# Rotary embedding on one core: storing each pair of batches in two halves of four rows

## The chip, the cores and the metric

One core of a Trainium2 chip. The metric is the device time of one execution in microseconds (us). The time of a run is 1.5 us more than its span in the profile, from the first to the last instruction (169.03 against 167.5 in the profile). Executions come in two states. A run is called slow when it is over 1.5% above the fastest of the same kernel; only fast runs are compared here. Ratios are the mean time of one kernel's fast runs over that of the other kernel's fast runs of the same rounds, so they are not quite the ratio of the medians that stand beside them.

Engines: PE is the matrix engine, DVE the vector engine, ACT the scalar engine, POOL the general one, SP the one that issues loads. "DMA engine" always means one of the 16 transfer engines.

## The reference

```python
batch, seq, dim = (16, 512, 1024)          # 16 heads of 64, float32
x = x.reshape(batch, seq, 16, 64)
x1, x2 = x[..., :32], x[..., 32:]
cos, sin = cos[None, :, None, :], sin[None, :, None, :]
out = np.concatenate([x1 * cos - x2 * sin, x1 * sin + x2 * cos], axis=-1)
```

33.55 MB come in and as much goes out; the arithmetic is two products and a sum per element.

## The kernel before

The work is cut into nine tiles: batch 0 alone (4 rows of 1024 numbers in each of 128 partitions), seven pairs of batches (8 rows), and batch 15 alone (4 rows). A row of a partition is 4 KB and the rows of a partition are contiguous in DRAM, so a pair moves as 128 descriptors (contiguous pieces) of 32 KB and a single batch as 128 of 16 KB. A transfer has landed when its semaphore has grown by 16, one for each DMA engine: the landing records of every transfer here have 16 entries. Five regions of 8 rows in on-chip memory are used in turn, so tile `t` is loaded into the region that tile `t - 5` has left.

```python
tiles = [(0, R1)] + [(b, R2) for b in range(1, batch - 1, 2)] + [(batch - 1, R1)]   # R1 = 4, R2 = 8
NT = len(tiles)
REGIONS = 5
...
loads = [(t, r, n) for t, (_, whole) in enumerate(tiles)
         for n in (R1 if t == 1 else whole,) for r in range(0, whole, n)]
...
def on_sync(sp):                                   # loads, in order
    for c, (t, r, n) in enumerate(loads):
        if t >= REGIONS:
            sp.wait_ge(sem_out[t - REGIONS], 16)   # the store that frees the region has landed
        sp.dma_start(in_sbuf(t, r, n), in_dram(x1, x2, t, r, n)).then_inc(sem_in[c], 16)
    ...                                            # (the two tables go behind the first load)
    sp.wait_ge(sem_rest, 16 * (NT - len(sem_out)))

def on_scalar(ae):                                 # copies of PE's sums, and stores
    ...
    for u in range(NU):
        t, r, k = where(u)
        if PE2[u]:
            ae.wait_ge(sem_e, n_pe[u])
            ae.activation(xs[:, k, :], t1_ps[:, u % NT1, :], COPY).then_inc(sem_a, 1)
        if r == tiles[t][1] - 1:                   # last row of the tile: store all of it
            wait_added(ae, u)
            ae.dma_start(in_dram(o1, o2, t, 0, r + 1), in_sbuf(t, 0, r + 1)).then_inc(
                sem_out[t] if t < len(sem_out) else sem_rest, 16)
```

Per row, POOL multiplies by the sine (`t2_sb`), DVE by the cosine (`t1_ps`), and DVE or PE adds them. Loads go out on SP's queue (`q1` in the profile), stores on ACT's queue (`q10`); while both hold work their packets take turns.

## Time and profile before

| | before |
|---|---|
| unprofiled runs | 161.96, 166.91, 161.80 us (median 161.96) |
| profiled run | slow state, 169.03 us, span 167.5 us |
| bytes | 67.26 MB, 402 GB/s over the span |
| POOL busy, DVE busy | 134.2 us, 131.0 us |

How to read it: POOL and DVE need some 132 us, the bytes need 156 us at the pace that the packets show, so the transfers set the length and what matters is whether the 16 DMA engines are ever without work.

### The profile page before, as it was taken

The numbers are of one execution on the slowest core, as the hardware profiler recorded it, in microseconds if no ns is written. First come the engines' busy times: TensorE is split into PE (matmuls) and PEld (weight loads), VectorE is DVE, ScalarE is ACT, GpSimd is POOL, SyncE is SP. The second block draws the span as 40 slices with busy tenths as digits, with TensorE's granted clock in tenths as the row PEclk, the third lists the DMA queues.
The fourth block names the chain that finished last, engine by engine and source line by source line (L and its number), as shares of the span: only waits on it lengthen the run. The fifth ranks groups of instructions, "written<-read, shape, count | busy, mean of one in ns | idle before, by whom it ended". The sixth has DMA issues, their size and how long they took to land.

```text
span 167.5 us, 565 instructions
## 1 busy us (share of the span) xinstructions
PE 70.2 (42%) x94; PEld 24.2 (14%) x94; DVE 131.0 (78%) x118; ACT 24.0 (14%) x26; POOL 134.2 (80%) x66
## 2 busy tenths in 40 slices
PE   6040039284937672476402907019390392700000
PEld 1020023022211211022101201013020130200000
DVE  0079996999999999999959994398964989999000
ACT  3020002211222040204020222002202022200000
POOL 5069999999999999999949994399954999996000
PEclk9999999855596789558985795855955559675555
DMA  5999999999899999999999999999999999488970
GB/s 160 420 425 431 474 423 387 438 434 446 384 485 384 479 391 470 385 470 407 446 415 430 438 391 477 399 462 407 470 399 419 427 470 415 172 376 376 442 317 23
DMA packets 3026, 67.26 MB, mean 402 GB/s; under 512 B 336, under 2 KB 592, under 8 KB 592
## 3 DMA queue, kind: packets, MB, share of 16 engines
q1 hardware_dynamic: 1728, 33.69, 47.6%
q10 hardware_dynamic: 1296, 33.56, 46.8%
q14 instruction: 2, 0.02, 0.0%
HBM read 33.69 MB, written 33.55 MB: 402 GB/s over the span
## 4 chain that ended last, share of the span: by engine, by line
DMA 48%; DVE 16%; POOL 11%; issue 7%; PE 7%; ACT 2%; SPq 0%; DVEq 0%; POOLq 0%
DMA x_sb<-in_x_dram 25%; DMA out_dram<-x_sb 19%; POOL t_sb L249 11%; DVE t_ps L285 8%; DVE x_sb L296 7%; PE t_ps L206 7%; DMA stage<-in_sin_dram 4%; ACT x_sb L171 2%; DVE t_sb L278 1%; SPq L155 0%; SPq L152 0%; ACT s_sb L161 0%; ACT s_sb L162 0%; POOLq L146 0%; DVEq L295 0%
## 5 line engine op out<-in xcount | busy, mean ns | idle before, releaser
L249 POOL TENSOR_TENSOR t_sb<-x_sb,s_sb 128x1024 f32<-128x1024 f32 x57 | 131.9, 2361 | 18.3 <-DMA x_sb<-in_x_dram 11.7
L206 PE MATMUL t_ps<-t_sb,ident 128*128 128x512 f32 x84 | 65.4, 935 | 68.9 <-POOL t_sb L249 48.6
L285 DVE TENSOR_TENSOR t_ps<-x_sb,pair_ps 128x1024 f32<-128x1024 f32 x56 | 67.5, 1222 | 14.4 <-DMA x_sb<-in_x_dram 11.0
L296 DVE TENSOR_TENSOR x_sb<-t_ps,t_sb 128x1024 f32<-128x1024 f32 x43 | 52.3, 1218 | 0.5 <-POOL t_sb L249 0.5
L206 PEld LDWEIGHTS t_ps<-t_sb,ident 128*128 128x128 f32 x84 | 22.3, 288 | 111.6 <-issue 59.6
L171 ACT ACTIVATE x_sb<-t_ps 128x1024 f32<-128x1024 f32 x21 | 21.5, 1024 | 113.2 <-PE t_ps L206 113.2
L285 DVE TENSOR_TENSOR t_ps<-x_sb,tab_ps 128x1024 f32<-128x1024 f32 x8 | 9.7, 1223 | 0.0
L278 DVE TENSOR_TENSOR t_sb<-x_sb,tab_ps 128x1024 f32<-128x1024 f32 x7 | 8.5, 1215 | 0.0
L256 DVE COPY tab_ps<-stage 128x128 f32<-128x128 f32 x1 | 0.3, 295 | 7.7 <-DMA stage<-in_cos_dram 7.7
L189 PE MATMUL pair_ps<-stage,pick 128*128 128x256 f32 x4 | 2.0, 667 | 5.2 <-DMA stage<-in_sin_dram 5.2
L182 PE MATMUL t_ps<-zero 128*128 128x512 bf16 x6 | 2.7, 630 | 1.3 <-DVE zero L254 1.3
L189 PEld LDWEIGHTS pair_ps<-stage,pick 128*128 128x128 f32 x4 | 1.2, 324 | 6.3 <-issue 6.1
L232 POOL TENSOR_SCALAR_AFFINE_SELECT pick<-pick 128x128 f32<-128x128 f32 x2 | 1.4, 706 | 0.1
L161 ACT ACT_TABLE_LOAD x1 | 1.3, 1283 | 0.8 <-PEq L329 0.8
L161 ACT ACTIVATE s_sb<-stage 128x128 f32<-128x128 f32 x1 | 0.3, 311 | 7.0 <-DMA stage<-in_sin_dram 7.0
L182 PEld LDWEIGHTS t_ps<-zero 128*128 128x128 bf16 x6 | 0.7, 137 | 2.4 <-DVE zero L254 1.2
L254 DVE MEMSET zero<- 128x256 uint32 x1 | 0.3, 272 | 0.9 <-PEq L329 0.9
L165 ACT ACTIVATE s_sb<-pair_ps 128x256 f32<-128x256 f32 x1 | 0.4, 384 | 1.7 <-PE pair_ps L189 1.7
L217 POOL MEMSET ident<- 128x128 f32 x1 | 0.2, 205 | 0.3 <-POOLq L329 0.3
L166 ACT ACTIVATE s_sb<-pair_ps 128x256 f32<-128x256 f32 x1 | 0.4, 377 | 0.0
L219 POOL TENSOR_SCALAR_AFFINE_SELECT ident<-ident 128x128 f32<-128x128 f32 x1 | 0.3, 297 | 0.1
L329 POOL MEMSET const-float32-0.0<- 128x1 f32 x1 | 0.1, 99 | 0.3 <-issue 0.3
(7 smaller groups left out, 1.3 us busy)
## 6 DMA issues: line engine op xcount, KB each, us to landing
out_dram<-x_sb ACTq DMA_DIRECT2D x7, 4096.0 KB, 31.9
x_sb<-in_x_dram SPq DMA_DIRECT2D x6, 4096.0 KB, 42.2
x_sb<-in_x_dram SPq DMA_DIRECT2D x4, 2048.0 KB, 13.8
out_dram<-x_sb ACTq DMA_DIRECT2D x2, 2048.0 KB, 15.8
stage<-in_cos_dram SPq DMA_DIRECT2D x1, 64.0 KB, 7.6
stage<-in_sin_dram SPq DMA_DIRECT2D x1, 64.0 KB, 7.3
```

The costliest lines, as they stand in the source:

```text
L161: ae.activation(s1_sb[:, :, 0, :], sv, COPY, scale=-1.0)
L165: ae.activation(s2[:, :, :, 0, :], pair_ps[:, :, 1, :, :], COPY, scale=-1.0)
L166: ae.activation(s2[:, :, :, 1, :], pair_ps[:, :, 1, :, :], COPY).then_inc(sem_s, 1)
L171: ae.activation(xs[:, k, :], t1_ps[:, u % NT1, :], COPY).then_inc(sem_a, 1)
L182: pe.matmul(t1_ps[:, k, b * BANK:(b + 1) * BANK], zero[:, 0:P], zero[:], start=True, stop=True).then_inc(sem_w, 1)
L189: pe.matmul(pair_ps[:, k].rearrange("p c r d -> p (c r d)"), pick[:, k].rearrange("q s b -> q (s b)"), stage[:].rearrange("q c f -> q (c f)"),
L206: ins = pe.matmul(t1_ps[:, u % NT1, b * BANK:(b + 1) * BANK], ident[:], t2[:, b * BANK:(b + 1) * BANK], start=False, stop=True, skip_group ...
L232: pl.affine_select(out=pick[:, k], in_=pick[:, k], compare_op=mybir.AluOpType.is_equal, fill=0.0, base=-k, pattern=[[-2, P // 2], [0, 2]], ...
L249: pl.tensor_tensor(t2_sb[:, u % NT2, :, :, :], swapped(k), over_heads(s_of(t, r)), mult).then_inc(sem_p, 1)
L278: ve.tensor_tensor(t2_sb[:, u % NT2, :, :, :], swapped(k), over_heads(v_ps), mult)
L285: ve.tensor_tensor(t1_ps[:, u % NT1, :].rearrange("p (h d) -> p h d", d=HALF), x_sb[:, k, :, :, :].rearrange("p h t d -> p (h t) d"), c_of ...
L296: ve.tensor_tensor(xs[:, k, :], t1_ps[:, u % NT1, :], t2_sb[:, u % NT2, :, :, :].rearrange("p h t d -> p (h t d)"), add,).then_inc(sem_v, 1)
```

## The change

Its intent is to let the first half of a pair leave while the second half is still being computed. The load of a pair stays one transfer with 32 KB descriptors.

```diff
                 if t >= REGIONS:
-                    sp.wait_ge(sem_out[t - REGIONS], 16)
+                    sp.wait_ge(sem_out[t - REGIONS], 16 * tiles[t - REGIONS][1] // R1)
...
-            sp.wait_ge(sem_rest, 16 * (NT - len(sem_out)))
+            sp.wait_ge(sem_rest, 16 * sum(n for _, n in tiles[len(sem_out):]) // R1)
...
-                if r == tiles[t][1] - 1:
+                if r % R1 == R1 - 1:
                     wait_added(ae, u)
-                    ae.dma_start(in_dram(o1, o2, t, 0, r + 1), in_sbuf(t, 0, r + 1)).then_inc(
+                    first = r + 1 - R1
+                    ae.dma_start(in_dram(o1, o2, t, first, R1), in_sbuf(t, first, R1)).then_inc(
                         sem_out[t] if t < len(sem_out) else sem_rest, 16
```

## The prediction

> **What bounds the kernel now.** I read the page first (busy shares, slices, queues), then the chain that ended last, then busy time by window, then the records of single DMA packets in the trace.
>
> ```profile
> PE 70.2 (42%) x94; PEld 24.2 (14%) x94; DVE 131.0 (78%) x118; ACT 24.0 (14%) x26; POOL 134.2 (80%) x66
> DMA  5999999999899999999999999999999999488970
> DMA packets 3026, 67.26 MB, mean 402 GB/s; under 512 B 336, under 2 KB 592, under 8 KB 592
> q1 hardware_dynamic: 1728, 33.69, 47.6%
> q10 hardware_dynamic: 1296, 33.56, 46.8%
> L249 POOL TENSOR_TENSOR t_sb<-x_sb,s_sb 128x1024 f32<-128x1024 f32 x57 | 131.9, 2361 | 18.3 <-DMA x_sb<-in_x_dram 11.7
> ```
>
> No engine is full: POOL 80%, DVE 78%. The 16 DMA engines are, in every slice but the last six. The store queue (q10) has 1296 packets: 9 stores of 128 partitions plus 16 completions is 9 x 144 = 1296, so **one packet is one row's descriptor**, 32 KB for a pair. In the packet records a 32 KB packet takes 1.213 us and a 16 KB one 0.611 us at the median, in either direction: 16 x 32768 B / 1.213 us = 432 GB/s for loads and stores together.
>
> ```profile
> 54.28 31.92 DMA out_dram<-x_sb
> 86.20 0.02 issue
> 86.22 41.54 DMA x_sb<-in_x_dram
> ```
>
> Columns are start, duration, what. The chain runs through a store of a pair, then the load that this store's landing releases (a region is reused five tiles later), and then POOL. 41.5 us for 4.2 MB is twice the 19.4 us that it needs at half the bandwidth, so it queued behind another load. From about 40 us on both queues are backlogged and alternate 1:1; landings of loads, and of stores, come some 20 us apart.
>
> ```profile
> 120.00:142.00 22.00, 10.19 (x12) 3.64 (x12) 17.63 (x16) 3.07 (x3) 17.83 (x9) 0.60 1.01 432
> 143.00:144.00 1.00, 1.00 (x2) 0.34 (x1) 1.00 (x2) 0.00 (x0) 1.00 (x1) 0.50 0.53 229
> 145.00:146.00 1.00, 0.53 (x2) 0.00 (x0) 1.00 (x2) 0.43 (x1) 1.00 (x1) 1.00 0.08 33
> 160.00:162.00 2.00, 0.00 (x0) 0.00 (x0) 0.00 (x0) 0.00 (x0) 0.00 (x0) 0.50 1.00 426
> 164.00:165.00 1.00, 0.00 (x0) 0.00 (x0) 0.00 (x0) 0.00 (x0) 0.00 (x0) 0.50 0.08 33
> ```
>
> The last two columns are the DMA share and GB/s. The reader is to see two holes, at 143 to 147 and after 163 us, in which the share is 0.08: **one engine of the 16** works while the others stand idle. The per-engine landings show it: 15 engines finish the load of the last pair by 122.5 us, one at 127.8; the last store by 163.1, one at 167.4. That engine's store packets took 1.25 to 1.85 us between 51 and 137 us; a lag of 3 us at 64 us grew to 9 us. But this profile is of the slow state (169.03 us; its span is 167.5, so 1.5 us lie outside). The fast runs took 161.8 and 161.96, and those count. I hold that the fast state is this picture without the late engine, which I can check: load of the last pair at 122.3, then 11 POOL rows at 2.31 (25.5 us) give 147.8, and the last store goes out at 149.2. The pair before it goes out at about 141.6, ahead of the end of the store in flight at 144.5 (its 15 good engines). So there is **no hole in the fast state**: 144.5 + 9.7 (8 packets of 1.213 of the last pair) + 4.9 (8 of 0.611) = 159.1, with 1.5 outside 160.6, against 161.8 measured.
>
> A second way gives the same. Packet durations summed over 16 engines are 158.2 us per engine; less some 0.6 us for the late engine, and started at 1.8 us, they end at 159.4, plus 0.3 for the landing and 1.5 outside: 161.2. The fast run is within 0.6 us of its DMA work.
>
> **What the Trainium skill says.** "DMA: Bandwidth & Descriptors", section "Queues, rings and completion order": each DMA engine goes round-robin between queue rows packet by packet, and finishes a packet before it switches. The trace agrees, with one descriptor to a packet: the first store (2 MB, 16 KB packets) ran beside 32 KB loads and landed at 39.4, 18.9 us after its issue; 8 turns of 0.611 + about 1.3 is 15.3 us plus some 2 of start. With equal bytes it would have been about 11.8. "Issuing engines are not separate DMA queues" says that all queues share the same 16 engines: here they sum to 432 GB/s, whichever runs. "Where 436 GB/s comes from" gives a ceiling of 435.2 GB/s; the 432 agree, so no arrangement of transfers can go much faster. "Why a DMA increments its semaphore by 16 and not by 1" warns of two DMAs in flight on one semaphore: only the total says that both landed. The change waits for that total (32), so a region still frees only when the second half has landed; no run shows the failure.
>
> **The change part by part.**
>
> Removed: seven stores of 128 descriptors of 32 KB. Added: fourteen of 16 KB. Bytes are the same. On each engine a pair's store goes from 8 x 1.213 = 9.70 us to 16 x 0.611 = 9.78, so 7 pairs cost 0.5 us more, all of it on the bound; seven more completions of 9 ns per engine are under 0.1. Seven more DMA issues on ACT at about 0.55 us are 3.9 us on an engine that is 14% busy; the first half is issued behind row 3, which ACT itself has just evacuated, so the wait there is met already. Path: 0.
>
> Moved, first: the first half of a pair goes out some 8 us earlier (half of a pair's 16.2 us on POOL). That gives DMA work earlier only where the store queue is empty.
>
> Moved, second: **the turns change**. While both queues are full, 32 KB of load alternate with 16 KB of store: loads get 2/3, 288 GB/s, stores 144. Worked forward: stores start at 20.5 with 7.7 MB loaded. The first store ends at 35, the first pair's at about 64; its landing releases the seventh tile's load at 64.5. The load of the sixth tile lands at about 74 (86 before), the seventh's at 89 (107), the last pair's at 105 (128), the last 2 MB at 120 (143). Compute then never starves: 9.7 + 131.9 us of POOL = 141.6, last store out at about 144 instead of 154.7. At 120 some 16.8 MB of stores are left, 39 us at 432 GB/s, each half computed before its turn. So DMA never runs dry, and the end is the sum of the DMA work again: about 159 us.
>
> Sum for the fast state: +0.6 for the smaller descriptors, between 0 and -0.6 for what is left of idle DMA: 161.8 + 0.6 - 0.3 = 162.1, rounded to **162.0 us**. The 11.7 us that POOL waits for loads disappear, and earn nothing: they were not what set the end.
>
> **Rivals.**
>
> 1. A real hole at the end that the early half fills. For: this profile's hole of 4 us at 143 and the tail of 4 us; if the fast state had them, 5 us (3%) would go, to 157. Against: during both, the late engine has work without a break (its landings of 152.9, 162.6 and 167.4 are 9.7 and 4.8 apart, exactly its packets), so even here it would end no sooner; and 157 less 1.5 outside is less than the 1.8 + 155.6 us that 67.26 MB at 432 GB/s take.
>
> 2. Stores at one third free the regions too late, loads run dry and compute starves: 165 or more. For: a region frees only after its second half, and each pair's store takes 29 us while loads compete. Against: when loads run dry stores alone get all 432 GB/s, so DMA stays busy; and by the working above the loads are 12 to 23 us earlier than before.
>
> 3. Mixed sizes disturb the engines. For: between 22 and 29 us, when the 16 KB store began beside 32 KB loads, about 40 load packets took 1.25 to 1.57 us instead of 1.21. If that lasted from 22 to 110 us it could cost 4 to 7 us, 166 to 169. Against: the same mix ran on to 38 us at 1.21.
>
> 4. A slow run as the median. One of three unprofiled runs was slow (166.9). The late engine's lag came from stores during compute; with fewer stores in that time it may shrink to some 6 us, 164 to 165, but it would not vanish.
>
> **Range and chances.** The ceiling of the bus forbids much below 160.5 and nothing in the work adds over 1 us, so 160.9 to 163.4 holds it, with the rest for rivals 3 and 4. Over 2% faster would be under 158.7, below the DMA work itself: 0.02. Over 2% slower, above 165.2, is rival 3 or a rival-2 error: 0.05. Within 2%: 0.93.
>
> **What the changed kernel's profile would show.** Right: POOL's wait for loads falls from 11.7 to under 3 us; the last load is issued near 110 instead of 107.5 but lands near 120 instead of 143; POOL's last row ends near 142 to 146 instead of 153; the last store takes longer to land (14 us or so, not 12.7), since it queues; the store queue has 9 x 128 + 7 x 128 + 16 x 16 = 2304 packets; DMA is full to the last slices in a fast profile; in a slow one a late engine remains. Wrong: a fast profile with idle DMA before the end, load packets well over 1.213 us throughout, ACT blocked in its DMA issues, or a total below 160.

## More of the kernel before

Tiles are counted from 0 in the code: t7 is the last pair, t8 the last single batch, and t8's load waits for t3's store.

SP's own waits say when a region came free. The rows of this view are: who waited for what, us in total, times, longest wait.

```profile
SPq L152 <- DMA out_dram<-x_sb: 100.4, 4, 33.9
SPq L156 <- DMA out_dram<-x_sb: 59.5, 1, 59.5
```

Four loads, those of t5 to t8, waited for a store: that is the link through which a change in the stores reaches the loads.

## The result, and the profile after

| | before | changed |
|---|---|---|
| median of 6 runs | 161.88 us (161.6 to 168.07) | 163.06 us (162.85 to 163.62) |
| slow runs among them | 2 | 0 |
| ratio of fast runs | | 1.0083 (1.0061 to 1.0105) |
| profile | slow, span 167.5 | fast, span 162.1 |

The change costs 0.8%: within 2%, and clearly not zero. From the page of the changed kernel:

```profile
DMA  5999999999999999999999999999999999999992
DMA packets 4034, 67.26 MB, mean 415 GB/s; under 512 B 448, under 2 KB 704, under 8 KB 704
q10 hardware_dynamic: 2304, 33.56, 48.5%
L250 POOL TENSOR_TENSOR t_sb<-x_sb,s_sb 128x1024 f32<-128x1024 f32 x57 | 131.7, 2356 | 6.6 <-ACT s_sb L162 6.6
```

The DMA row is full from the second slice to the last but one: no hole. The store queue has 2304 packets, one per descriptor and completion. POOL's wait for loads, 11.7 us in the slow profile before, has gone from its row; what is left is the 6.6 us at the start for the tables. Now the end of the chain (start, duration, what):

```profile
139.24 1.22 DVE t_ps L286
140.46 1.05 DVE x_sb L297
141.51 0.04 issue
141.55 1.23 DVE x_sb L297
```

The chain stops at 142.8 us, because it follows instructions back and the last one is a vector addition. The span is 162.1: **for 19 us only the store queue works**, and the chain is silent about it. In such a kernel the end has to be read from the windows. The columns are the window, its length, busy time of PE, its weight loads, DVE, ACT and POOL, the granted clock, the DMA share and GB/s:

```profile
158.00:159.00 1.00, 0.00 (x0) 0.00 (x0) 0.00 (x0) 0.00 (x0) 0.00 (x0) 0.50 0.88 377
159.00:160.00 1.00, 0.00 (x0) 0.00 (x0) 0.00 (x0) 0.00 (x0) 0.00 (x0) 0.50 0.16 66
160.00:161.00 1.00, 0.00 (x0) 0.00 (x0) 0.00 (x0) 0.00 (x0) 0.00 (x0) 0.50 0.08 33
161.00:162.00 1.00, 0.00 (x0) 0.00 (x0) 0.00 (x0) 0.00 (x0) 0.00 (x0) 0.50 0.04 16
```

Most of the 16 engines stop before 160; one or two go on at 33 GB/s and less to 161.7. The last store's landing records run from 159.3 to 162.0 us, and the span ends with the last of them, so the last two microseconds belong to **the lag of the latest engine**.

The profile of before was slow, so it could not be compared with this one. The first experiment that mattered was therefore the kernel before again, in a fast run (161.93 us, span 160.4; all fast runs of that kernel lie between 161.4 and 162.1). Its POOL row and four windows:

```profile
L249 POOL TENSOR_TENSOR t_sb<-x_sb,s_sb 128x1024 f32<-128x1024 f32 x57 | 131.9, 2363 | 13.1 <-DMA x_sb<-in_x_dram 6.7 <-ACT s_sb L162 6.4
143.00:147.00 4.00, 0.00 (x0) 0.00 (x0) 4.00 (x4) 0.00 (x0) 4.00 (x3) 0.52 1.12 483
158.00:159.00 1.00, 0.00 (x0) 0.00 (x0) 0.00 (x0) 0.00 (x0) 0.00 (x0) 0.50 0.73 311
159.00:160.00 1.00, 0.00 (x0) 0.00 (x0) 0.00 (x0) 0.00 (x0) 0.00 (x0) 0.50 0.04 16
160.00:161.00 1.00, 0.00 (x0) 0.00 (x0) 0.00 (x0) 0.00 (x0) 0.00 (x0) 0.50 0.00 0
```

There is no hole at 143 to 147 in the fast state (483 GB/s; windows this short count a packet at its edges, so single values swing about the mean of some 430). What took its place at the end is small: the engines stop between 159.0 and 160.3.

So the comparison is reduced to two numbers that the landing records of the last store give, one per engine: when the **median** engine is done, and how much later the **latest** one is.

| profile | median engine, us | latest engine, us | lag, us | span, us |
|---|---|---|---|---|
| before, fast (b_same2) | 159.19 | 160.33 | 1.13 | 160.4 |
| changed | 159.57 | 162.03 | 2.46 | 162.1 |
| changed, again (a_same) | 159.57 | 161.31 | 1.74 | 161.3 |

The median engine is 0.38 us later, the latest one 1.0 to 1.7 us. Most of what the change costs is lag. (There is one profile of the fast state of before, and two of the change.)

### The profile page after: what moved, and what is told of

Its sections match the earlier page's. It is cut to its first block, busy times and chain, and to the rows that moved or that the text cites. A ratio compares the mean times of both kernels' runs of the same rounds, so it can differ in the third digit from the quotient of the medians.

```text
span 162.1 us, 579 instructions
## 1 busy us (share of the span) xinstructions
PE 68.3 (42%) x94; PEld 23.2 (14%) x94; DVE 130.7 (81%) x118; ACT 23.9 (15%) x26; POOL 134.1 (83%) x66
## 2 busy tenths in 40 slices
DMA packets 4034, 67.26 MB, mean 415 GB/s; under 512 B 448, under 2 KB 704, under 8 KB 704
## 3 DMA queue, kind: packets, MB, share of 16 engines
q10 hardware_dynamic: 2304, 33.56, 48.5%
## 4 chain that ended last, share of the span: by engine, by line
POOL 26%; DVE 21%; issue 17%; PE 15%; DMA 5%; ACT 4%; SPq 0%; POOLq 0%; DVEq 0%
POOL t_sb L250 26%; PE t_ps L207 15%; DVE t_ps L286 11%; DVE x_sb L297 9%; DMA stage<-in_sin_dram 5%; ACT x_sb L171 3%; DVE t_sb L279 1%; SPq L155 0%; SPq L152 0%; ACT s_sb L161 0%; ACT s_sb L162 0%; POOLq L146 0%; POOLq L144 0%; DVEq L296 0%; DVEq L283 0%
## 5 line engine op out<-in xcount | busy, mean ns | idle before, releaser
L250 POOL TENSOR_TENSOR t_sb<-x_sb,s_sb 128x1024 f32<-128x1024 f32 x57 | 131.7, 2356 | 6.6 <-ACT s_sb L162 6.6
L207 PE MATMUL t_ps<-t_sb,ident 128*128 128x512 f32 x84 | 63.5, 908 | 57.5 <-POOL t_sb L250 33.1
L207 PEld LDWEIGHTS t_ps<-t_sb,ident 128*128 128x128 f32 x84 | 21.3, 279 | 99.7 <-DVE t_ps L286 57.5
```

The lines of the kernel that those rows point to most:

```text
L207: ins = pe.matmul(t1_ps[:, u % NT1, b * BANK:(b + 1) * BANK], ident[:], t2[:, b * BANK:(b + 1) * BANK], start=False, stop=True, skip_group ...
L250: pl.tensor_tensor(t2_sb[:, u % NT2, :, :, :], swapped(k), over_heads(s_of(t, r)), mult).then_inc(sem_p, 1)
```

## The experiments

Theory going in: the DMA engines are full in both kernels, and the change costs packet size. Rivals: a hole at the end that the early half fills; the early start itself; the unequal turns of loads and stores. A further one was tested: the lag of an engine that falls behind at a certain moment.

### Controls: both kernels again (b_same, b_same2, a_same)

No edit.

> The kernel before, unchanged: a control, and a chance of a profile in the fast state. Theory (the fast run is full of DMA work): ratio 1.000 within 0.3%, and in a fast profile no window before 157 us with less than 400 GB/s, span about 160. Rival (a hole at the end also in the fast state): a fast profile shows some 3 us with the DMA share under 0.5 near 143.

> The kernel before once more, for a profile in the fast state. Theory (in fast runs the DMA engines are full and the end is the DMA work plus the lag of the latest engine): last store's landing on the median engine at 159 to 159.8, on the last engine near 160.3, no hole at 143. Rival (a hole in fast runs too): idle DMA of over 1 us before 157.

> The changed kernel once more: does one late engine come back in each run? Theory (the change costs 0.5 us of packet size and some 0.8 us of an engine that falls behind in the stores near 115 us): 1.008 again, profile with some 16 KB store packets near 1.2 us between 114 and 118 us and one engine about 2 us behind at the end. Rival (a single disturbance of that run): profile with all engines within 1 us at the end, span 160.5 to 161.

Measured: b_same 0.9996 (0.9974 to 1.0018), but four of its six runs and its profile were slow. b_same2 gave the fast profile shown above, with a median engine at 159.19. Short windows before 157 us do fall below 400 GB/s, against what was expected (382 at 140 to 143, 371 at 147 to 150), but the packet records have 15 to 20 packets in flight at every moment from 3.2 to 158.6 us: there is no hole. a_same 1.0069 (1.0056 to 1.0082), so the loss is real and repeats. Its store packets between 114 and 118 us were slow again, which is taken up below.

### Only the last pair in halves (last_pair)

```diff
-                if r == tiles[t][1] - 1:
+                n = R1 if t == NT - 2 else tiles[t][1]
+                if r % n == n - 1:
                     wait_added(ae, u)
+                    first = r + 1 - n      # (the transfer starts there, n rows long; the end waits for one more)
```

> Only the last pair's store in halves, all other stores at 32 KB as before: tests the hole at the end by itself. Theory: there is none in fast runs, 1.000 (0.998 to 1.003), POOL waits for loads as before, about 11 us. Rival (a hole of 1 us or more): 0.99 or less.

Measured: 0.9996 (0.9977 to 1.0015); its profile was slow. Filling the place where a hole would be earns nothing in fast runs. That rival is out.

### Two halves, but both issued at the end of the pair (late_halves)

```diff
-                if r % R1 == R1 - 1:
+                if r == tiles[t][1] - 1:
                     wait_added(ae, u)
-                    first = r + 1 - R1
-                    ae.dma_start(...)
+                    for first in range(0, r + 1, R1):
+                        ae.dma_start(...)
```

> Stores in 16 KB halves as in the change, but both issued after the pair's last row: size and turns of the change without the early start. Theory (the cost is packet size, the early start earns nothing): the same as the change, 1.008, POOL waits under 3 us for loads. Rival (the early start costs by contention or earns something): differs from the change by over 0.4%.

Measured: 1.0078 (1.0050 to 1.0107), the same as the change. POOL did not wait for loads here either, and the latest engine was again 2.2 us behind. So the early start, which was the intent of the change, neither earns nor costs: all of the difference comes with the smaller transfers.

### Loads in halves too (both16)

```diff
-    loads = [... for n in (R1 if t == 1 else whole,) for r in range(0, whole, n)]
+    loads = [... for n in (R1,) for r in range(0, whole, n)]      # on top of the change
```

> Loads in 16 KB halves too (each with its own semaphore), stores as in the change: turns 1:1 again, packets all small. Theory: another 0.5 us for smaller load packets over the change, 1.011 to 1.013; loads land later again and POOL waits for them for 5 to 12 us, which earns or costs nothing. Rival (the 2:1 turns are what costs): back to 1.003 or less.

Measured: 1.0015 (1.0004 to 1.0027), six runs between 162.10 and 162.16. **The theory failed here.** With twice as many small packets the kernel loses less than the change does. The median engine is near where the theory puts it (159.82, 0.63 later than before, where the packet times add up to some 0.9 for small packets in both directions), but the lag is only 0.74. Packet size is a small, real term; the rest of the change's loss is something that equal turns do not have. POOL waited 7.1 us for loads, and that cost nothing, as expected.

### Stores in quarters (quarters)

```diff
+    Q = 2                                  # in place of R1 in the change's five lines
```

> Stores in four quarters of 8 KB packets: the suspected costs doubled, turns 4:1. Theory packet size: 8 KB in about 0.31 us, so 1.0 us over the change, 1.014. Theory turns (unequal turns make an engine late): more than that, 1.015 to 1.03. Rival (neither): as the change, 1.008.

Measured: 1.0186 (1.0164 to 1.0208), more than size alone gives. An 8 KB packet took 0.309 us, so four cost 1.236 us against 1.222 for two of 16 KB: over seven pairs with 8 partitions per engine, and with the two single tiles, about 0.9 us more than the change. Measured were 1.8 us more (164.75 against 162.95 for a_same in the same rounds). The engines now spread over 160.0 to 162.8 at the last store (median 160.67, 1.1 later than in the change, lag 2.1), and store packets of up to twice their length appear, here at 76 to 79 and 98 to 99 us.

### The turns reversed (load16)

```diff
-    loads = [... for n in (R1 if t == 1 else whole,) ...]
+    loads = [... for n in (R1,) ...]       # on the kernel before: stores stay whole, 32 KB
```

> Loads in 16 KB halves, stores whole at 32 KB: turns 1:2, the change turned round; size cost the same 0.5 us. Theory: stores win, regions free early, but loads land late, POOL waits for them for 12 us or more, and a hole opens before the last stores: 1.02 to 1.05. Rival (only bytes and packet sizes count): 1.003 to 1.008.

Measured: 1.0447 (1.0433 to 1.0460). Size costs no more here than in the change, so this is the turns. With 16 KB loads against 32 KB stores the loads get a third (138 GB/s beside 288 for the stores, in the packet records from 42 to 56 us), and the profile shows what the change's own turns protect from:

```profile
L249 POOL TENSOR_TENSOR t_sb<-x_sb,s_sb 128x1024 f32<-128x1024 f32 x57 | 132.0, 2361 | 23.0 <-DMA x_sb<-in_x_dram 14.8
140.00:143.00 3.00, 0.35 (x1) 0.38 (x2) 2.66 (x3) 0.00 (x0) 3.00 (x3) 0.50 0.95 410
144.00:146.00 2.00, 2.00 (x3) 0.33 (x1) 0.00 (x0) 0.00 (x0) 0.80 (x1) 0.50 0.27 115
146.00:150.00 4.00, 0.40 (x1) 0.00 (x0) 1.20 (x2) 1.02 (x1) 1.16 (x1) 0.92 0.06 25
150.00:155.00 5.00, 0.00 (x0) 0.00 (x0) 5.00 (x6) 0.00 (x0) 5.00 (x3) 0.51 0.66 282
```

The first number after the bar in POOL's row is busy time, then the mean of one in ns, then 23.0 us idle, 14.8 of them for loads. The stores have caught up with the computation, the last loads have only just landed, and between 144 and 155 us DMA has little to do while POOL and DVE first wait for the last loads and then compute. That hole costs some 7 us. All 16 engines end within 0.2 us of each other here. A late one can catch up in the hole, which would explain it; no run tests that apart, but dry16, below, has a hole before the last store too, and no lag.

### Where the lag comes from (half_release, late_release, dry16)

The packet records of the changed kernel show 16 KB stores of up to twice their usual 611 ns, all within 3 us. Each entry is start in us and duration in ns, for store packets over 800 ns:

```
changed          115.1/925  115.3/988  116.0/1218  116.3/1208  117.3/1208
changed, again   114.9/1076 115.1/809 115.2/1091 115.7/1208 115.9/1208 116.0/1208 116.4/1208
late_halves      96.4/953  114.7/808  115.6/1191  116.8/1208
half_release     none
late_release     124.1/931 124.3/980 124.4/874 124.6/1159 125.1/1206 125.2/1219 125.3/1221
                 125.3/976 125.7/1204 126.3/1208 126.5/1208 126.5/1208 127.0/1208
```

At that time, in the changed kernel, the load queue starts again after a pause. The load of t7 has run out (its last packet starts at 109.7). The load of t8 is issued only at 111.9, when t3's second half has landed, and its first packet starts at 115.5. Two edits move that moment. SP's issues between 90 and 125 us show it (start of the first, time until the end of the second, which is t8's): the changed kernel, half_release, late_release.

```profile
92.53 19.70 SPq L152 DMA_DIRECT2D x_sb<-in_x_dram  x2
92.34 6.34 SPq L155 DMA_DIRECT2D x_sb<-in_x_dram  x2
92.42 29.45 SPq L155 DMA_DIRECT2D x_sb<-in_x_dram  x2
```

half_release: t8 has 4 rows and needs only the first half of its region, so its load can go when t3's *first* half has landed. That half gets a semaphore of its own.

```diff
+                if t == NT - 1:
+                    sp.wait_ge(sem_half, 16)
-                if t >= REGIONS:
+                elif t >= REGIONS:
                     sp.wait_ge(sem_out[t - REGIONS], 16 * tiles[t - REGIONS][1] // R1)
...
+                    if t == NT - 1 - REGIONS and first == 0:
+                        sem = sem_half     # (and the end also waits for t3's second half)
```

> The change, with the last load released by the first half of the fourth tile's store (some 12 us earlier), so that the load queue has no pause before it. Theory (an engine falls behind when the load queue, run dry, starts again beside 16 KB stores): no store packets near 1.2 us between 110 and 120 us, latest engine within 1 us of the median one, 1.002 to 1.004. Rival (16 KB stores make engines late anyway): 1.007 to 1.009 as the change.

Measured: **1.0002** (0.9988 to 1.0016), six runs between 161.71 and 161.93. The load was issued at 98.4 us and followed the one before it without a pause (110.9). The end of its profile, to be laid beside the four windows of the changed kernel above:

```profile
158.00:159.00 1.00, 0.00 (x0) 0.00 (x0) 0.00 (x0) 0.00 (x0) 0.00 (x0) 0.50 0.76 328
159.00:160.00 1.00, 0.00 (x0) 0.00 (x0) 0.00 (x0) 0.00 (x0) 0.00 (x0) 0.50 0.08 33
160.00:161.00 1.00, 0.00 (x0) 0.00 (x0) 0.00 (x0) 0.00 (x0) 0.00 (x0) 0.50 0.00 0
```

The median engine is at 159.53, as in the change (159.57), and the latest at 160.22, a lag of 0.70 instead of 1.7 to 2.5. Sizes, turns and early halves are those of the change; this pause alone is gone, and the loss with it. The ratio is even below the 1.002 to 1.004 expected: the lag is 0.4 us less than in the fast profile of before, about what the smaller packets cost.

late_release holds the same load back further, until t4's store has landed.

```diff
                     sp.wait_ge(sem_out[t - REGIONS], 16 * tiles[t - REGIONS][1] // R1)
+                if t == NT - 1:
+                    sp.wait_ge(sem_half, 16)      # incremented by t4's second half
```

> The change, with the last load held back further, until the fifth tile's store has landed (near 121 us, some 9 us later than in the change): the load queue stays dry for longer and starts again at another time. Theory (in this kernel the restart makes an engine late): slow 16 KB store packets move from 115 to about 3 us after the new issue, one engine 1.5 to 2.5 us late at the end, 1.007 to 1.010. Rival (something at 115 us itself, not the restart): no slow packets or again near 115, engines within 1 us, 1.002 to 1.004. The last store would still go out before its turn, so no hole is expected.

Measured: 1.0082 (1.0049 to 1.0114). The load was issued at 121.5 and its first packet started at 125.0. The slow stores moved with it, from 115 to 124 to 127 us, and the lag at the end was 2.45 us. Five engines landed after 160.5, against two in the first profile of the change; the windows show it as a higher share. POOL waited 5.3 us for this load. The median engine was at 159.51, so the longer pause opened no hole:

```profile
159.00:160.00 1.00, 0.00 (x0) 0.00 (x0) 0.00 (x0) 0.00 (x0) 0.00 (x0) 0.50 0.39 164
160.00:161.00 1.00, 0.00 (x0) 0.00 (x0) 0.00 (x0) 0.00 (x0) 0.00 (x0) 0.50 0.19 82
```

The landing records of all the transfers show when the lag arises. In the changed kernel the latest engine was 1.1 us behind the median one for the store whose median landing is at 110.8, 1.8 for that at 115.8 and 2.5 for that at 125.5, and it stayed 2.4 to 2.5 behind for the seven stores after it. In late_release the lag was 0.8 at 120.6, 2.9 at 125.6, and 2.4 to 2.5 from then on; in half_release it was 0.9 at 120.6 and 0.7 from then on. What was lost at the restart was not made up by the end.

The load queue of the change pauses once before, from 89.0 to 96.4 us, and half_release keeps that pause. No store packet was slow at that restart, and the lag that it made (2.0 to 3.2 us for the store at 96.4 in these three runs) was down to 0.9 to 1.4 at the next store. So not every restart does harm.

dry16 makes the same pause in the kernel that has none (both16).

```diff
                     sp.wait_ge(sem_out[t - REGIONS], 16 * tiles[t - REGIONS][1] // R1)
+                if t == NT - 1:
+                    sp.wait_ge(sem_half, 16)      # on both16, incremented by t5's second half
```

> All packets 16 KB (the run with loads in halves too, 1.0015), but the last load held back until the sixth tile's store has landed, near 133 us: the load queue runs dry and starts again beside 16 KB stores. Theory (restart of a dry load queue makes an engine late): store packets near 1.2 us some 3 us after that issue, an engine 1.5 to 2.5 us late, 1.007 to 1.012. Rival (the pause is harmless): 1.001 to 1.004; a late start of the last store beyond 155 us would blur it and shows in the chain.

Measured: 1.0160 (1.0145 to 1.0175), but not for the reason expected. No store packet was slow at the restart (issued at 131.7, first packet at 135.2). The last store was issued only at 156.3, so no packet was in flight from 155.5 to 157.2, as the expectation had warned; all engines then ended within 0.15 us. **The theory in its general form fails**: a restarted load queue beside 16 KB stores is not enough. In the changed kernel the second restart is what makes the engines late, shown from both sides; what else must be present stays open. The depth of the store backlog does not explain it alone: five halves were issued and not landed at the restart that did harm, four at the first, harmless one, three in dry16. Over the seven profiles with 14 restarts of a paused load queue beside stores of 16 or 8 KB, every store packet of 1.5 times its usual length or more starts within 2 us of a restart's first load packet, but only 7 of the restarts have any. The same shape is seen with the queues exchanged: at 22 to 29 us, when the store queue first starts beside a full load queue, some 37 load packets were slow in the change (1.25 us and more instead of 1.213), as in the kernel before.

## Why the prediction was right or wrong

The time (162.0 predicted, 163.06 measured) lay inside the range and "within 2%" held. Point by point:

1. **The fast state of before has no hole.** Right. The working put the last store's landing at 159.1; the fast profile has the median engine at 159.19, and last_pair earned nothing.
2. **Turns of 2:1, loads early, compute never starved.** Right in kind: between 42 and 88 us the packet records have 285 GB/s of loads beside 144 of stores. The loads of the sixth and seventh tile were worked out to 74 and 89 us and landed at 73.8 to 75.6 and 88.3 to 90.1. Those of the last pair and the last batch were put at 105 and 120 and landed at 110.8 to 111.7 and 125.3 to 128.2. Two things were missed. The last pair's region came free at 92.5 us, 3.5 us after the load queue had run dry. And a load issued to a dry queue took 3.6 to 3.9 us to its first packet (92.5 to 96.4, 111.9 to 115.5), where the working let it move bytes at once. That could be read beforehand: in the profile before, the first store was issued at 20.5 and its first packet started at 24.0, not "some 2" later, and it landed at 39.4, not at the 35 of the working. POOL's waits for loads went to nothing, the last row was done by 142.8, and the gain was nil, as stated.
3. **Packet size.** Right in kind: "+0.6 for the smaller descriptors" was 0.38 on the median engine.
4. **The term that was mis-sized** is the other half of the sum: "between 0 and -0.6 for what is left of idle DMA". It has the wrong sign. What is left in the fast run before is 1.1 us by which one engine ends after the median one, and the change does not shrink that, it raises it to 1.7 to 2.5. That is 0.6 to 1.3 us in place of a credit of 0.3, and it, not the packet size, is most of the 1.2 us between the medians.
5. **Rival 2** said that loads would run dry, and was answered with "DMA stays busy". Both are true, and the answer was still too short: busy on average is not enough where the end waits for the latest of 16 engines. half_release shows that the second pause was worth the whole loss.
6. **Rival 3**: the slow 32 KB loads at 22 to 29 us are in the profiles of before and of the change alike (38 and 37 packets), and did not spread with the mixed sizes of the change: 6 came after 30 us, against 4 before. **Rival 4**: no slow run came up among the changed kernel's.
7. "The last store takes longer to land (14 us or so)": 19.2 us, from 142.9 to 162.0. 1.1 us of the difference is that it was issued before the worked-out 144, and 2.5 is the lag: its median engine landed at 159.57.

The version that the experiments point to, half_release, equals the kernel before (1.0002); nothing tried beats it in fast runs. With the median engine at 159.2 us in the fast profile and 67.26 MB at 432 GB/s taking 155.7 us, there is little to win by rearranging transfers.

## What to carry to other kernels

Where the transfer engines never rested, as here, moving a store earlier earned nothing, and compute's waits for loads were free; count bytes over packet pace first. Then look at who ends last: the last store here landed with its latest engine, so compare the median engine's landing with the latest one's before explaining a difference of a microsecond. And where a transfer is split, think of splitting its release as well: a load that needs half a region can wait for half a store. Here that kept its queue from running dry, and was worth the 0.8%.

## What the Trainium skill lacked or had wrong

- "DMA: Bandwidth & Descriptors", "Queues, rings and completion order": it gives 9 to 17 descriptors as typical for a packet. Here every descriptor of 8, 16 or 32 KB is a packet (1296, 2304 and 4608 packets on the store queue). The page does not draw the consequence that the **descriptor sizes set the shares** of two full queues: 138 GB/s of loads beside 288 of stores with 16 KB loads and 32 KB stores (4.5% slower), 285 beside 144 the other way round (0.8%).
- The same page, "Latency and other measured facts", gives about 600 ns to the first byte for transfers issued from SP or ACT. At the start of the kernel it was 1.0 us from issue to first packet (0.80 to 1.81), but on a dry queue beside a full one 3.5 to 3.9 us (92.5 to 96.4, 111.9 to 115.5; late_release 121.5 to 125.0).
- No page has it: beside such a restart, 16 KB store packets took up to 1.22 us instead of 0.611 for up to 3 us, and from then on the latest engine stayed 1.7 to 2.5 us behind the median one to the end. The cause is open (half of the restarts, that of dry16 among them, had no slow packet).
- No page has it: over all rounds the kernel before, b_same included, was slow in 20 of 56 runs (last_pair in 3 of 7, load16 in none of 5, both with 32 KB stores), and the seven kernels whose stores all have packets of 16 KB or less in none of 47. In its slow profiles 32 KB store packets took up to 1.89 us and one engine ended 3.8 to 4.4 us after the median one. This is a count, not an explanation, and no claim about fast runs rests on it.
